# A decoder layer on one core: residual kept with its channels on the partitions up to the router, output projection with the weights stationary, half of the second shift and scale computed on VectorE

## The chip, the core and the metric

One core of a Trainium2 chip runs the whole layer for 256 tokens in one launch. Its engines are TensorE (PE, matrix products into the accumulator memory PSUM; its weight loads are listed as PEld), VectorE (DVE), ScalarE (ACT), GpSimd (POOL) and SyncE (SP, which here only issues transfers). Each runs its own instructions in a fixed order and waits for the others by semaphores. The metric is the device time of one execution in microseconds.

## What is computed

```python
mod = silu(c) @ w_ada + b_ada                      # 2048 -> 6 x 2048
sh1, sc1, g1, sh2, sc2, g2 = split(mod, 6)
h = rmsnorm(x, norm1_g) * (1 + sc1) + sh1          # x: 256 x 2048, f32
proj = h @ w_in                                    # 2048 -> 4928
o_a = hgrn2(...)                                   # gated recurrence, 8 heads, chunks of 64
o_b = latent_attention(...)                        # 8 heads, low-rank q and kv, causal
mix = concat(o_a, o_b) @ w_out                     # 2048 -> 2048
x = x + g1 * mix
h2 = rmsnorm(x, norm2_g) * (1 + sc2) + sh2
y = moe(h2)    # top 1 of 4 groups, top 2 of 8 experts in it; silu(h2 @ gate) * (h2 @ up) @ down
x = x + g2 * y
```

All inputs and weights are f32. Products on the way to the router are made as three products of rounded parts (hi x hi, hi x lo, lo x hi), each weight tile being split into a rounded part and a rest on the chip.

## The kernel before

**Weights.** All large weights come as chunks of up to 2 MB (128 partitions x 4096 columns) through one ring of slots, in one order that is written down as a list of items (lines 104 to 132). `ring_fill` (line 172) issues the next chunk on SP whenever a slot is free. The ring has four slots at first, two more after the second output-projection item (`close_temps`), and one more when the split buffers are given back. The items in order: chunks of w_ada for the first shift and scale (`ad1`, then `adt`) between those of w_in (`wh`, `win`), low-rank weights (`qup`, `kvup`), w_out (`wout`, two halves of the contraction by four blocks of 512 columns), and 192 expert chunks. The 32 chunks of w_ada for g1, sh2, sc2 and g2 (`ada`) are strewn between the last w_in items and the w_out items: `SPREAD` says how many go behind each, and what is left at the end (three chunks of g2) goes behind the first two expert chunks (`HEAD`).

**Shift and scale.** An `ada` chunk is multiplied on PE, with one column of silu(c) stationary, into four rows of one accumulator (line 293, tile `pada`, 16 matmuls a chunk). `ada_end` turns a finished row into columns on the partitions by four transposes (`pcol`), or adds it to a row (line 302, `brows`) for g1 and g2; g1 then goes out to memory and back to be broadcast over the partitions into `gate`. An `adt` chunk holds transposed weights: DVE multiplies it by silu(c), broadcast in `gate`, and sums along the row (line 271, two instructions of 128x2048 per chunk, each overwriting the chunk's half).

**First norm.** x is loaded with tokens on the partitions (four tiles of 512 channels by two blocks of tokens). `norm1` sums squares along the row, makes one reciprocal root per token (tile `sm`) and scales x by this column (line 337). `make_h` transposes 256 channels at a time on PE (`pxT`, line 382), applies shift and scale on ACT as per-partition operands (`h`, line 385) and splits the result into `hhi` and `hlo` (lines 388, 389).

**Products.** `dense` (line 411) takes for each 128 rows of weights one of four split buffers: ACT writes the rounded part (line 417), DVE the rest (line 418). Then PE runs, by default, six matmuls with activations stationary and 512 weight columns streaming (lines 432 to 434), into one PSUM bank per block of tokens; in the `turned` form, used for some w_in blocks, twelve matmuls with 128 weight columns stationary and 256 tokens streaming (lines 425 to 427), whose results have channels on the partitions. Each call takes two of the four PSUM banks with the tag "w" (tile `pacc`).

**Recurrence and attention.** `hgrn(0)` and `hgrn(1)` handle four heads each; their outputs go through transposes (`pmt`) into the two parts `mhi` and `mlo` of the output projection's input. `ptr` on PE waits for `d` (line 513), a step of the recurrence on DVE.

**Output projection.** `w_out` runs eight items of eight k-tiles. The first half's results are copied to `mix0` (line 578); the second half adds to it, multiplies by g1 and adds to x (lines 582 to 584), which was loaded again. `x2_ready` squares the result, transposes it on PE (`px2T`) and multiplies it by the router's weights (line 640, `plog`), which `router_weights` has scaled by the second norm's gain and scale; the shift enters by a sum of 16 products on 36 columns (line 614).

**Router and experts.** After the last item come the reciprocal root, the logits (line 879), the choice of experts on small tiles, their ranks by matmuls (`prank`), and the gather of tokens by one-hot matmuls (`pgat`, line 970). Then each round takes 32 token slots of an expert through gate/up (`pgu`, line 1040) and down (`py`, line 1016).

An order of all instructions on each engine is made when the kernel is built; `high_priority(-120)` at line 270 sets the 128x2048 products back behind other work in it.

## Time and profile before

| | us |
|---|---|
| runs | 1504.66, 1507.17, 1507.49 (median 1507.17) |
| the profiled execution | 1505.27 |
| its span in the trace | 1503.0 |
| first matmul of the input projection | 31.46 |
| last matmul of the output projection begins | 545.20 |
| first expert matmul | 571.41 |

Some 2.3 us of the execution lie outside the span. Over the span PE is busy for 75%, DVE for 39%, ACT for 23%, and 575.6 MB move at 383 GB/s; these are means over stages of different kinds. Busy times of PE overlap in the trace (the end of a matmul is modelled), so the distance between starts says more than the length of one. [...]

### The profile page before, as it was taken

Reading aid. Unit: us, or ns where it says so; the run is one execution under the profiler, and the core shown is the slowest. Engines: PE = TensorE matmul, PEld = TensorE weight load, DVE = VectorE, ACT = ScalarE, POOL = GpSimd, SP = SyncE. Lnnn points to the kernel's source line nnn. Section 1 sums busy time; section 2 is a strip of 40 time slices with the busy share of each in tenths; the row PEclk is TensorE's granted clock in tenths of the full one; section 3 lists DMA queues with packets and bytes.
Section 4 is the critical chain, followed back from the end, with each engine's and each line's share of the span. In section 5 each row is a group of like instructions: output and inputs, shape, how many; then the busy total and the mean of one; then the engine's idle time right before and its main releaser. Section 6 shows DMA issues by size and latency. Waiting matters only on the chain.

```text
span 1503.0 us, 22846 instructions
## 1 busy us (share of the span) xinstructions
PE 1127.9 (75%) x9893; PEld 687.8 (46%) x9893; DVE 588.6 (39%) x1200; ACT 338.4 (23%) x699; POOL 5.0 (0%) x9
## 2 busy tenths in 40 slices
PE   5989999979999989675666666657657756666556
PEld 2868887737568756333323323323423423332222
DVE  4699998769765552220120121113112112112112
ACT  5634446536435423000100100100100100000000
POOL 0000000000000000000000000000000000000000
PEclk7999999989999999888888888879888889779787
DMA  9788796877979798999999999999999999999995
GB/s 373 263 332 356 298 352 257 315 302 313 369 293 376 293 373 343 430 429 430 430 430 430 430 430 429 429 431 430 430 430 430 430 431 430 430 429 429 431 430 222
DMA packets 44143, 575.61 MB, mean 383 GB/s; under 512 B 4858, under 2 KB 5114, under 8 KB 8712
## 3 DMA queue, kind: packets, MB, share of 16 engines
q1 hardware_dynamic: 42496, 570.56, 91.4%
q10 hardware_dynamic: 1544, 3.56, 0.6%
q8 instruction: 79, 1.29, 0.3%
q14 instruction: 24, 0.20, 0.0%
HBM read 572.00 MB, written 2.11 MB: 382 GB/s over the span
## 4 chain that ended last, share of the span: by engine, by line
DMA 51%; PE 37%; DVE 9%; ACT 1%; issue 1%; SPq 0%; ACTq 0%; DVEq 0%
DMA wch<-in_w_gu_dram 37%; DMA wch<-in_w_down_dram 13%; PE pgu L1040 5%; PE pacc L433 5%; PE pacc L434 5%; PE pacc L432 5%; PE pada L293 3%; PE py L1016 3%; PE pcmb L993 2%; PE pgat L970 2%; DVE wch L271 2%; DVE split L418 2%; DVE proj L457 1%; PE pacc L427 1%; PE pacc L425 1%; PE pacc L426 1%
## 5 line engine op out<-in xcount | busy, mean ns | idle before, releaser
L1040 PE MATMUL pgu<-wch,XT 128*32 128x256 f32 x4096 | 309.7, 455 | 201.0 <-DMA wch<-in_w_gu_dram 201.0
L1040 PEld LDWEIGHTS pgu<-wch,XT 128*32 128x32 f32 x4096 | 139.2, 126 | 361.0 <-DMA wch<-in_w_gu_dram 253.9
L1016 PE MATMUL py<-wch,hT 128*32 128x256 f32 x2048 | 167.9, 485 | 76.8 <-DMA wch<-in_w_down_dram 72.1
L1020 DVE TENSOR_TENSOR Y<-py,gate 32x256 f32<-32x256 f32 x256 | 107.6, 420 | 216.5 <-PE py L1016 213.6
L1005 DVE TENSOR_TENSOR hid<-sgu,pgu 128x128 f32<-128x128 f32 x32 | 9.2, 287 | 462.2 <-ACT sgu L1003 462.2
L418 DVE TENSOR_TENSOR split<-wch,split 128x512 fp32r<-128x512 f32 (+2 forms) x248 | 159.5, 666 | 69.6 <-ACT split L417 69.0
L417 ACT ACTIVATE split<-wch 128x512 fp32r<-128x512 f32 (+2 forms) x248 | 148.0, 614 | 161.2 <-PE pacc L434 98.4
L1016 PEld LDWEIGHTS py<-wch,hT 128*32 128x32 f32 x2048 | 78.9, 133 | 155.0 <-issue 60.8
L1003 ACT ACTIVATE sgu<-pgu 128x128 f32<-128x128 f32 x32 | 8.9, 277 | 602.5 <-PE pgu L1040 602.5
L975 ACT ACTIVATE XT<-pgat,sh,a 128x128 f32<-128x128 f32 x128 | 48.1, 456 | 223.1 <-PE pgat L970 223.0
L433 PE MATMUL pacc<-split,hhi 128*128 128x512 f32 (+1 forms) x192 | 75.5, 393 | 7.0 <-DVE split L418 7.0
L425 PE MATMUL pacc<-hhi,split 128*128 128x256 f32 x256 | 72.4, 286 | 2.8 <-ACT hhi L388 2.2
L426 PE MATMUL pacc<-hlo,split 128*128 128x256 f32 x256 | 72.7, 285 | 1.7 <-DVE hlo L389 1.7
L434 PE MATMUL pacc<-split,hlo 128*128 128x512 f32 (+1 forms) x192 | 73.7, 386 | 0.0
L432 PE MATMUL pacc<-split,hhi 128*128 128x512 f32 (+1 forms) x192 | 72.9, 392 | 0.8 <-DVE proj L457 0.7
L427 PE MATMUL pacc<-hhi,split 128*128 128x256 f32 x256 | 72.2, 285 | 1.1 <-DVE split L418 1.1
L293 PE MATMUL pada<-wch,ca 128*1 128x512 f32 x512 | 68.7, 602 | 3.3 <-DVE pada L288 3.3
L993 PE MATMUL pcmb<-Y,pwt 128*128 128x512 f32 x128 | 59.2, 605 | 15.5 <-DVE Y L1020 15.5
L970 PEld LDWEIGHTS pgat<-ohr,x 128*128 128x128 f32 x512 | 63.4, 205 | 10.7 <-issue 9.8
L970 PE MATMUL pgat<-ohr,x 128*128 128x128 f32 x512 | 66.8, 291 | 0.7 <-DVE sm L937 0.7
L271 DVE SCALAR_TENSOR_TENSOR wch<-wch,gate 128x2048 f32<-128x2048 f32 x24 | 54.8, 2284 | 0.0
L457 DVE TENSOR_TENSOR proj<-proj,pacc 128x512 f32<-128x512 f32 (+1 forms) x80 | 51.2, 662 | 0.8 <-PE pacc L434 0.4
(311 smaller groups left out, 1215.4 us busy)
## 6 DMA issues: line engine op xcount, KB each, us to landing
wch<-in_w_gu_dram SPq DMA_DIRECT2D x128, 2048.0 KB, 31.1
wch<-in_w_down_dram SPq DMA_DIRECT2D x64, 2048.0 KB, 31.5
wch<-in_w_ada_dram SPq DMA_DIRECT2D x36, 2048.0 KB, 10.1
wch<-in_w_ada_t_dram SPq DMA_DIRECT2D x12, 2048.0 KB, 7.9
wch<-in_w_in_dram SPq DMA_DIRECT2D x12, 2048.0 KB, 9.2
wch<-in_w_out_dram SPq DMA_DIRECT2D x8, 2048.0 KB, 9.5
wch<-in_w_in_h_dram SPq DMA_DIRECT2D x8, 1024.0 KB, 8.9
wch<-in_w_in_dram SPq DMA_DIRECT2D x3, 1664.0 KB, 7.0
```

Source lines behind the costliest of these rows:

```text
L293: PE.matmul(acc[b][32 * j:32 * j + 1, :], ca[:, kt:kt + 1], w[:, o:o + 512], start=kt == 0, stop=kt == 15)
L417: S.activation(s[:, 0, :ncol], w, AF.Copy)
L418: V.tensor_sub(s[:, 1, :ncol], w, s[:, 0, :ncol])
L426: PE.matmul(o, s[:, 0, c], lo, start=False, stop=False, skip_group_check=True)
L432: PE.matmul(o, hi[:, c], s[:, 0, :ncol], start=first, stop=False)
L433: PE.matmul(o, hi[:, c], s[:, 1, :ncol], start=False, stop=False)
L434: PE.matmul(o, lo[:, c], s[:, 0, :ncol], start=False, stop=stop)
L970: PE.matmul(ps[:, 128 * i:128 * i + 128], x2[kt // 4][:, t, 128 * (kt % 4):128 * (kt % 4) + 128], ohr[:, t], start=t == 0, stop=t == 1)
L993: PE.matmul(ps, PWT[G4][:, 128 * t:128 * t + 128], Y4[j // 2][:, 512 * (j % 2):512 * (j % 2) + 512], start=True, stop=True)
L1016: PE.matmul(py[32 * j:32 * j + 32, :256], H["T"][:, 32 * kt:32 * kt + 32], w[:, 1024 * kt + 256 * j:1024 * kt + 256 * j + 256], start=kt = ...
L1020: V.tensor_mul(Y[q][r:r + 32, 256 * j:256 * j + 256], py[32 * j:32 * j + 32, :256], gate[32 * j:32 * j + 32, c:c + 256])
L1040: PE.matmul(gu[32 * j:32 * j + 32, :256], XT[G4][kt // 8][:, kt % 8, 32 * e4:32 * e4 + 32], w[:, 1024 * i + 256 * j:1024 * i + 256 * j + 2 ...
```

## The change

x comes transposed (`xT`), so that channels lie on the partitions from the load to the router. `norm1` squares on ACT and DVE, adds the four tiles up, sums over the partitions by two matmuls with a tile of ones, and multiplies x by a row of reciprocal roots, broadcast along the free dimension. `make_h` has no transposes left and works in place.

The output projection uses the `turned` form. After each item, of either half, four instructions (line 581 of the new kernel) take 256 columns each from PSUM, multiply by g1 (now a column per channel block) and add to the residual `xt`, which is loaded in the first half. `mix0`, the broadcast g1 and the trip of g1 through memory are gone.

Of sh2 and sc2, channels 0 to 1023 are computed on PE as before, as eight chunks `m2` that hold both; channels 1024 to 2047 come as eight transposed chunks `at2`, each multiplied on DVE by two instructions of 128x2048, and stand last in the list: two behind the first w_out item, one behind each of the next six. The g2 chunks stand before them, and none is left behind the experts. The router's weights are scaled, and its shift summed, in four steps of four k-tiles.

The sum of squares for the second norm is made on ACT and DVE and finished by ten small matmuls into the logits' bank. The rows of x2, which the gather and the end need, are rebuilt by 32 transposes and eight ACT copies after the logits (`x2_rows`).

Lines left out, removed ones for the most part, are marked by "...".

```diff
-SPREAD = (1, 4, 7, 5, 5, 2, 0, 0, 0, 2, 1, 1, 0)
+SPREAD = (1, 4, 7, 5, 5, 3, 1, 1, 1, 1, 1, 1, 0)
-HEAD = 2
...
-    mods = [("ada", b, ch) for b in ("g1", "sh2", "sc2", "g2") for ch in range(8)]
+    mods = [("ada", b, ch) for b in ("g1", "m2", "g2") for ch in range(8)] + [("at2", kt) for kt in range(8, 16)]
-    g2 = list(late_mods)
+    assert not list(late_mods)
-    items += experts[:HEAD] + g2 + experts[HEAD:]
+    items += experts
...
-    xx = [tmp([P, 2, 512], "x") for _ in range(4)]
+    xx = [tmp([P, 4, 256], "x") for _ in range(4)]
-        nc.sync.dma_start(xx[j], A["x"][:, :, 512 * j:512 * j + 512])
-    ring["limit"] = 1
+        nc.sync.dma_start(xx[j], A["xT"][:, 4 * j:4 * j + 4])
+    ring["limit"] = 3
...
+    def adt_chunk(it, sh, a, b, gain):
+        w = ring_get(it)
+        i = it[1]
         r = sm(2, "adt")
         for k in range(2):
             wk = w[:, 2048 * k:2048 * k + 2048]
             with tc.high_priority(-120):
                 V.scalar_tensor_tensor(wk, wk, 1.0, gate, op0=OP.mult, op1=OP.mult, accum_out=r[:, k:k + 1])
...
+        ring_done(it)
+        mod_shift(sh[:, i:i + 1], r[:, 0:1], b + i, 1)
+        mod_scale(a[:, i:i + 1], r[:, 1:2], b + 16 + i, gain + i, 1)
     def ada_end(b):
...
+        if b == "g2":
             for j in range(4):
                 V.tensor_add(brow[32 * j:32 * j + 1], brow[32 * j:32 * j + 1], acc[b][32 * j:32 * j + 1])
...
+            return
+        S.activation(rows, acc[b], AF.Copy)
+        pt = pm("pcol")
+        for i in range(4):
+            PE.transpose(pt[:, 128 * i:128 * i + 128], rows[:, 128 * i:128 * i + 128], ident)
+        t = sm(16)
+        V.tensor_copy(t.rearrange("p (j s) -> p s j", j=4), pt.rearrange("p (s q) -> p s q", s=4)[:, :, 0:128:32])
+        if b == "g1":
+            mod_shift(g1, t, P_BA + 64, 16)
         else:
...
+            mod_shift(sh2[:, 0:8], t[:, 0:8], P_BA + 32, 8)
+            mod_scale(a2[:, 0:8], t[:, 8:16], P_BA + 48, P_N2, 8)
+    def norm1():
+        sq = [big([P, 1024], "sq") for _ in range(4)]
+        flat = [x.rearrange("p a b -> p (a b)") for x in xx]
+        for j in range(4):
+            if j < 2:
+                S.activation(sq[j], flat[j], AF.Square)
             else:
...
+                V.tensor_mul(sq[j], flat[j], flat[j])
+        V.tensor_add(sq[0], sq[0], sq[1])
+        V.tensor_add(sq[2], sq[2], sq[3])
+        V.tensor_add(sq[0], sq[0], sq[2])
+        V.tensor_add(sq[1][:, :512], sq[0][:, :512], sq[0][:, 512:])
+        ps = pm("pss")
+        for i in range(2):
+            PE.matmul(ps[:, :256], ones, sq[1][:, 256 * i:256 * i + 256], start=i == 0, stop=i == 1)
+        ms, y, t = sq[2][:, 0:256], sq[2][:, 256:512], sq[2][:, 512:768]
+        V.tensor_scalar(ms, ps[:, :256], 1.0 / D, EPS, op0=OP.mult, op1=OP.add)
+        S.activation(t, ms, AF.Ln)
+        S.activation(y, t, AF.Exp, scale=-0.5)
+        V.tensor_mul(t, y, y)
+        V.tensor_mul(t, t, ms)
+        V.tensor_scalar(t, t, -0.5, 1.5, op0=OP.mult, op1=OP.add)
+        V.tensor_mul(y, y, t)
         for j in range(4):
...
+            for r in range(2):
+                v = xx[j][:, 2 * r:2 * r + 2]
+                V.tensor_mul(v, v, bc(y[:, None, :], [P, 2, 256]))
     posf = sm(2)
...
-        h32 = tmp([P, 2, 256], "h32")
-        ps = pm("pxT")
-        for i in range(2):
-            for t in range(2):
-                c = 256 * i + 128 * t
-                d0 = 128 * (2 * r + i)
-                PE.transpose(ps[:, c:c + 128], xx[q][:, t, d0:d0 + 128], ident)
+        sl = slice(2 * r, 2 * r + 2)
-            S.activation(h32[:, i], ps[:, 256 * i:256 * i + 256], AF.Identity, scale=a1[:, kt:kt + 1],
-                         bias=sh1[:, kt:kt + 1])
-        sl = slice(2 * r, 2 * r + 2)
-        S.activation(hi[:, sl], h32, AF.Copy)
-        V.tensor_sub(lo[:, sl], h32, hi[:, sl])
+            h = xx[q][:, 2 * r + i]
+            S.activation(h, h, AF.Identity, scale=a1[:, kt:kt + 1], bias=sh1[:, kt:kt + 1])
+        S.activation(hi[:, sl], xx[q][:, sl], AF.Copy)
+        V.tensor_sub(lo[:, sl], xx[q][:, sl], hi[:, sl])
...
             return hi[:, kt % 4], lo[:, kt % 4]
         def end(ps):
...
+            for h in range(4):
+                m = xt[j][:, h]
+                V.scalar_tensor_tensor(m, ps[h // 2][:, 256 * (h % 2):256 * (h % 2) + 256], g1[:, 4 * j + h:4 * j + h + 1],
+                                       m, op0=OP.mult, op1=OP.add)
+            if half:
+                xt_ready(j)
+        if half == 0:
+            xt[j] = big([P, 4, 256], "xt")
+            nc.sync.dma_start(xt[j], A["xT"][:, 4 * j:4 * j + 4])
+        dense(ring_get(it), 512, range(8), lhs, end, turned=True)
         ring_done(it)
...
+    xt, x2 = {}, {}
     wr2 = {}
     def router_load():
         wr2["w"] = big([P, 16, 36], "wr")
         S.dma_start(wr2["w"], A["w_r"])
+        v = cpool.tile([P, 36], F32, name="rv")
+        V.memset(v, 0.0)
+        wr2["v"] = v
+        wr2["t"] = []
     def router_begin():
         wr2["ps"] = pm("plog")
...
+    def router_weights(q):
+        wr, v = wr2["w"], wr2["v"]
+        if q % 2 == 0:
+            wr2["t"].append(big([P, 8, 128], "wr2"))
+            G.memset(wr2["t"][-1], 0.0)
+        k = slice(4 * q, 4 * q + 4)
+        V.tensor_mul(wr2["t"][q // 2][:, 4 * (q % 2):4 * (q % 2) + 4, :36], wr[:, k], bc(a2[:, k, None], [P, 4, 36]))
+        for kt in range(4 * q, 4 * q + 4):
             V.scalar_tensor_tensor(v, wr[:, kt], sh2[:, kt:kt + 1], v, op0=OP.mult, op1=OP.add)
+        if q < 3:
+            return
         ps = pm("prb")
         PE.matmul(ps[:, :36], ones, v, start=True, stop=True)
         rb = cpool.tile([P, 36], F32, name="rb")
         V.tensor_add(rb, ps[:, :36], pr[:, R_B:R_B + 36])
         wr2["b"] = rb
...
+    def xt_ready(j):
         for i in range(4):
             kt = 4 * j + i
             for t in range(2):
...
+                PE.matmul(wr2["ps"][:, 128 * t:128 * t + 128], xt[j][:, i, 128 * t:128 * t + 128], wr2["t"][kt // 8][:, kt % 8],
                           start=kt == 0 and t == 0, stop=kt == 15, skip_group_check=True)
+        if j < 3:
+            sq = big([P, 4, 256], "sq2")
+            S.activation(sq, xt[j], AF.Square)
+            if j == 0:
+                wr2["sq"] = sq
+                return
+            V.tensor_add(wr2["sq"], wr2["sq"], sq)
+            if j == 2:
+                s = wr2["sq"]
+                V.tensor_add(s[:, 0:2], s[:, 0:2], s[:, 2:4])
+                V.tensor_add(s[:, 0], s[:, 0], s[:, 1])
+            return
+        s = wr2["sq"]
+        for i in range(3):
+            S.activation(s[:, 1 + i], xt[j][:, i], AF.Square)
+        sq = big([P, 256], "sq2")
+        V.tensor_mul(sq, xt[j][:, 3], xt[j][:, 3])
+        ps = wr2["ps"]
+        for i in range(5):
+            for t in range(2):
+                PE.matmul(ps[:, 256 + t:257 + t], (s[:, i] if i < 4 else sq)[:, 128 * t:128 * t + 128], ones[:, 0:1],
+                          start=False, stop=i == 4, skip_group_check=True)
+    def x2_rows(j):
+        x2[j] = big([P, 2, 512], "x2")
+        for t in range(2):
+            ps = pw("px2")
+            for i in range(4):
+                PE.transpose(ps[:, 128 * i:128 * i + 128], xt[j][:, i, 128 * t:128 * t + 128], ident)
+            S.activation(x2[j][:, t], ps, AF.Copy)
     def mla_pre():
         qa, kva = proj.pop(0), proj.pop(1)
...
-        ("ada", "sc2", 7): router_weights,
+        ("ada", "m2", 7): lambda: (router_weights(0), router_weights(1)),
+        ("at2", 11): lambda: router_weights(2),
+        ("at2", 15): lambda: router_weights(3),
...
-    V.tensor_reduce(ms, ss2.rearrange("p (t j) -> p t j", t=2), AX.X, OP.add)
-    V.tensor_scalar(ms, ms, 1.0 / D, EPS, op0=OP.mult, op1=OP.add)
+    V.tensor_scalar(ms, wr2["ps"][:, 256:258], 1.0 / D, EPS, op0=OP.mult, op1=OP.add)
+    for j in range(4):
+        x2_rows(j)
...
-    for it in g2:
-        ada_chunk(it[1], it[2])
```

**VectorE at the start.** Rows of before, from the last step of the reciprocal root (L202) on; `x` are the four tiles, `sh` and `a` the first shift and scale, `pcol` the columns that PE made of the first two chunks:

```order
L202 TENSOR_TENSOR sm_173<-sm_173,sm_175 128x2
L337 TENSOR_SCALAR x_89<-x_89,sm_173 128x512 x2
L337 TENSOR_SCALAR x_90<-x_90,sm_173 128x512 x2
L337 TENSOR_SCALAR x_91<-x_91,sm_173 128x512 x2
L337 TENSOR_SCALAR x_92<-x_92,sm_173 128x512 x2
L418 TENSOR_TENSOR split_221<-wch_104,split_221 128x512
...
L277 TENSOR_TENSOR sh_131<-pcol_33_199,pc 128x2
L280 TENSOR_TENSOR a_132<-pcol_33_199,pc 128x2
L249 MEMSET pad_49_279 128x512
L281 SCALAR_TENSOR_TENSOR a_132<-a_132,pc 128x2
```

The same place after; `pss` is the sum over the partitions, L344 the last step of the reciprocal root, L348 the multiplication by its row:

```order
L338 TENSOR_SCALAR sq_156<-pss_166 128x256
...
L344 TENSOR_TENSOR sq_156<-sq_156 128x256
L422 TENSOR_TENSOR split_211<-wch_103,split_211 128x512
L348 TENSOR_TENSOR x_91<-x_91,sq_156 128x512 x2
L348 TENSOR_TENSOR x_92<-x_92,sq_156 128x512 x2
L348 TENSOR_TENSOR x_93<-x_93,sq_156 128x512 x2
L348 TENSOR_TENSOR x_94<-x_94,sq_156 128x512 x2
L283 TENSOR_TENSOR sh_134<-pcol_25_195,pc 128x2
L286 TENSOR_TENSOR a_135<-pcol_25_195,pc 128x2
L422 TENSOR_TENSOR split_226<-wch_103,split_226 128x512
L287 SCALAR_TENSOR_TENSOR a_135<-a_135,pc 128x2
```

The multiplication stands in both ahead of `sh` and `a`; the root's steps have grown from 2 to 256 columns, and all but one split stand behind it.

**VectorE between the first and the second output-projection item.** Before: from the last step of `mlo`, the input's second part, to the first splits of the second item (`wch_3862`):

```order
L470 SCALAR_TENSOR_TENSOR mlo_3799<-pmt_3807,pc,mhi_3798 128x4x128
L288 MEMSET pada_3991 128x512
L314 COPY sm_3959<-pcol_3954 128x4x4
L618 TENSOR_TENSOR rb<-prb_3987,pr 128x36
L280 TENSOR_TENSOR a_134<-sm_3959,pc 128x16
L281 SCALAR_TENSOR_TENSOR a_134<-a_134,pc 128x16
L609 TENSOR_TENSOR wr_679_3963<-wr_2821,a_134 128x8x36
...
L418 TENSOR_TENSOR split_4005<-wch_3862,split_4005 128x512
L418 TENSOR_TENSOR split_4014<-wch_3862,split_4014 128x512
```

After: `wch_3818` and `wch_3828` are the first two `at2` chunks, `pada_3507` is the accumulator of g2, `pacc_3832` and `pacc_3833` are the banks of the first item, `split_3994` is the second item's first:

```order
L474 SCALAR_TENSOR_TENSOR mlo_3765<-pmt_3773,pc,mhi_3764 128x4x128
L277 SCALAR_TENSOR_TENSOR wch_3818,adt_3974<-wch_3818,gate 128x2048 x2
L307 TENSOR_TENSOR brow_105<-brow_105,pada_3507 1x512 x4
L283 TENSOR_TENSOR sh_136<-adt_3974,pc 128x1
L286 TENSOR_TENSOR a_137<-adt_3974,pc 128x1
L277 SCALAR_TENSOR_TENSOR wch_3828,adt_3982<-wch_3828,gate 128x2048
L581 SCALAR_TENSOR_TENSOR xt_3830<-pacc_3832,g_138,xt_3830 128x256 x2
L581 SCALAR_TENSOR_TENSOR xt_3830<-pacc_3833,g_138,xt_3830 128x256 x2
...
L277 SCALAR_TENSOR_TENSOR wch_3828,adt_3982<-wch_3828,gate 128x2048
L615 SCALAR_TENSOR_TENSOR rv<-wr_2769,sh_136,rv 128x36
...
L422 TENSOR_TENSOR split_3994<-wch_3958,split_3994 128x512
```

Four 128x2048 instructions, the adds that finish g2 and the first item's four multiply-adds now stand ahead of the second item's splits; before, small steps did.

**VectorE at the fifth item** (second half, first block). After; `wch_4129` is its weights, `pacc_4141` and `pacc_4142` are the banks of the third item, which the fifth uses again, and `wch_4134` is an `at2` chunk:

```order
L422 TENSOR_TENSOR split_4425<-wch_4129,split_4425 128x512
L422 TENSOR_TENSOR split_4440<-wch_4129,split_4440 128x512
L422 TENSOR_TENSOR split_4455<-wch_4129,split_4455 128x512
L422 TENSOR_TENSOR split_4470<-wch_4129,split_4470 128x512
L613 TENSOR_TENSOR wr_689_4277<-wr_2769,a_137 128x4x36
L277 SCALAR_TENSOR_TENSOR wch_4134,adt_4561<-wch_4134,gate 128x2048
L581 SCALAR_TENSOR_TENSOR xt_4139<-pacc_4141,g_138,xt_4139 128x256 x2
L581 SCALAR_TENSOR_TENSOR xt_4139<-pacc_4142,g_138,xt_4139 128x256 x2
L283 TENSOR_TENSOR sh_136<-adt_4561,pc 128x1
L277 SCALAR_TENSOR_TENSOR wch_4134,adt_4561<-wch_4134,gate 128x2048
```

Before, the eight splits of this item stand in a row without anything between them, and ACT emptied the banks. Now the banks of the third item are emptied behind four splits of the fifth and one 128x2048 instruction.

## Rows read from the trace of the kernel before

**Rows 1.** Windows by stage: window, length, busy time (instructions) by engine, clock, DMA share, GB/s

```profile
0.00:31.50 31.50, 15.75 (x53) 4.66 (x53) 15.89 (x53) 15.41 (x30) 1.16 (x5) 0.82 0.92 361
...
126.00:213.00 87.00, 85.29 (x545) 75.59 (x547) 84.28 (x137) 40.16 (x67) 0.00 (x0) 1.00 0.83 321
...
449.70:545.60 95.90, 95.84 (x480) 72.06 (x480) 50.95 (x78) 41.54 (x73) 0.00 (x0) 1.00 0.86 342
...
545.60:571.40 25.80, 20.32 (x119) 11.64 (x116) 15.13 (x60) 6.70 (x20) 0.00 (x0) 0.80 0.83 336
...
571.40:1503.00 931.60, 607.97 (x6801) 305.62 (x6800) 172.02 (x387) 65.69 (x190) 0.00 (x0) 0.85 0.98 420
```

**Rows 2.** Timeline of SP around 555: start, time, queue, line, tile, issues

```profile
554.96 22.62 SPq L172 DMA_DIRECT2D wch<-in_w_gu_dram  x3
```

**Rows 3.** Timeline of startup: start us, length us, engine, line, operation, count, idle before

```profile
16.77 0.63 ACT L328 ACTIVATE junk<-x 128x512 f32<-128x512 f32 x1 [0.30 <-DMA x<-in_x_dram]
...
21.35 3.26 DVE L337 TENSOR_SCALAR x<-x,sm 128x512 f32<-128x512 f32 x8
...
29.73 1.02 ACT L385 ACTIVATE h<-pxT,sh,a 128x256 f32<-128x256 f32 x2 [1.60 <-DVE a L281]
...
31.46 0.80 PE L425 MATMUL pacc<-hhi,split 128*128 128x256 f32 x2 [2.25 <-ACT hhi L388]
```

**Rows 4.** Groups by form, 432 to 571.4: busy us, mean ns, idle before, releaser

```profile
L418 DVE TENSOR_TENSOR split<-wch,split 128x512 fp32r<-128x512 f32 x63 | 43.0, 689 | 40.4 <-ACT split L417 40.4
...
L417 ACT ACTIVATE split<-wch 128x512 fp32r<-128x512 f32 x61 | 38.2, 631 | 52.3 <-PE pacc L434 49.0 <-issue 2.6 <-DVE split L418 0.7
...
L582 DVE TENSOR_TENSOR mix<-mix,pacc 128x512 f32<-128x512 f32 x8 | 5.3, 682 | 2.1 <-PE pacc L434 2.1
...
L302 DVE TENSOR_TENSOR brows<-brows,pada 1x512 f32<-1x512 f32 x4 | 2.7, 684 | 0.7 <-PE pada L293 0.6
...
L556 DVE TENSOR_TENSOR o<-o,sm 128x1024 f32<-128x1024 f32 x1 | 1.2, 1224 | 0.0
```

**Rows 5.** Costliest groups of the whole span (page, part 5)

```profile
L1040 PE MATMUL pgu<-wch,XT 128*32 128x256 f32 x4096 | 309.7, 455 | 201.0 <-DMA wch<-in_w_gu_dram 201.0
...
L1020 DVE TENSOR_TENSOR Y<-py,gate 32x256 f32<-32x256 f32 x256 | 107.6, 420 | 216.5 <-PE py L1016 213.6
```

**Rows 6.** Timeline of PE from the last projection matmul to the gather

```profile
545.52 4.45 PE L293 MATMUL pada<-wch,ca 128*1 128x512 f32 x34
...
549.90 1.09 PE L632 MATMUL px2T<-cst,x 128*128 128x128 f32 x8
...
551.89 2.05 PE L640 MATMUL plog<-wr,x2T 128*128 128x128 f32 x16
...
566.02 5.46 PE L970 MATMUL pgat<-ohr,x 128*128 128x128 f32 x32 [0.66 <-DVE sm L937]
```

**Rows 7.** Groups by form, 126 to 213: the products of ada chunks on VectorE

```profile
L271 DVE SCALAR_TENSOR_TENSOR wch<-wch,gate 128x2048 f32<-128x2048 f32 x13 | 29.7, 2284 | 0.0
```

**Rows 8.** Waits of PE, 31.4 to 432: total us, times, longest us

```profile
PE pmt L824 <- DVE o L818: 5.4, 2, 4.6
...
PE ptr L520 <- DVE d L513: 5.1, 1, 5.1
```

**Rows 9.** Window behind the wait of pmt, columns as in the first group

```profile
309.00:315.00 6.00, 2.68 (x12) 1.63 (x16) 5.80 (x9) 3.38 (x4) 0.00 (x0) 0.50 0.96 406
```

**Rows 10.** Windows of equal length, instructions of the tile pacc alone

```profile
455.00:466.20 11.20, 11.20 (x50) 9.02 (x49) 0.00 (x0) 1.20 (x2) 1.00 0.98 394
...
127.00:138.20 11.20, 11.20 (x97) 11.20 (x96) 2.00 (x4) 0.00 (x0) 1.00 0.81 310
```

**Rows 11.** Timeline around the second output-projection item, PE and then DVE

```profile
444.49 1.90 PE L293 MATMUL pada<-wch,ca 128*1 128x512 f32 x16
...
447.23 0.48 DVE L288 MEMSET pada<- 128x512 f32 x1 [6.06 <-ACT rows L309]
...
449.28 2.49 DVE L418 TENSOR_TENSOR split<-wch,split 128x512 fp32r<-128x512 f32 x4
```

More of the change, by code (lines that the diff above doesn't have):

```diff
@@ L94, in tile_hybrid_layer @@
     ident = cst[:, C_ID:C_ID + 128]
-    ones = cst[:, C_ONE:C_ONE + 128]
+    ones = cpool.tile([P, 128], F32, name="ones")
+    G.memset(ones, 1.0)
     tri64 = cst[:, C_TRI64:C_TRI64 + 128]
@@ L145, in source @@
         if k == "ada":
-            return A["w_ada"][("g1", "sh2", "sc2", "g2").index(it[1]), it[2]], 4096
+            return A["w_ada"][("g1", "m2", "g2").index(it[1]), it[2]], 4096
+        if k == "at2":
+            return A["w_ada_t2"][it[1] - 8], 4096
         if k == "win":
@@ L241, in tile_hybrid_layer @@
     a2 = cpool.tile([P, 16], F32, name="a2")
+    g1 = cpool.tile([P, 16], F32, name="g1")
     def ad1_chunk(h, c):
@@ L574, in end @@
         def end(ps):
-            if half == 0:
-                mix0[j] = big([P, 2, 512], "mix0")
-                for t in range(2):
-                    S.activation(mix0[j][:, t], ps[t], AF.Copy)
-                return
-            m = mix0.pop(j)
-            for t in range(2):
-                V.tensor_add(m[:, t], m[:, t], ps[t])
-                V.tensor_mul(m[:, t], m[:, t], gate[:, 512 * j:512 * j + 512])
-                V.tensor_add(x2[j][:, t], x2[j][:, t], m[:, t])
-            x2_ready(j)
-        if half:
-            x2[j] = big([P, 2, 512], "x2")
-            nc.sync.dma_start(x2[j], A["x"][:, :, 512 * j:512 * j + 512])
-        dense(ring_get(it), 512, range(8), lhs, end)
+            for h in range(4):
[8 more added lines that the diff above has]
+        dense(ring_get(it), 512, range(8), lhs, end, turned=True)
         ring_done(it)
-    x2, mix0 = {}, {}
-    ss2 = cpool.tile([P, 8], F32, name="ss2")
+    xt, x2 = {}, {}
     wr2 = {}
@@ L850, in tile_hybrid_layer @@
         elif it[0] == "adt":
-            adt_chunk(it[1])
+            adt_chunk(it, sh1, a1, P_BA, P_N1)
+        elif it[0] == "at2":
+            adt_chunk(it, sh2, a2, P_BA + 32, P_N2)
         elif it[0] == "ada":
@@ L948, in gate_rows @@
             ps = pw("pg2")
-            PE.matmul(ps, ones[32 * j:32 * j + 1, :], brows[32 * j:32 * j + 1, 1], start=True, stop=True, tile_position=(32 * j, 0))
+            PE.matmul(ps, ones[32 * j:32 * j + 1, :], brow[32 * j:32 * j + 1], start=True, stop=True, tile_position=(32 * j, 0))
             S.activation(gate[:, 512 * j:512 * j + 512], ps, AF.Copy)
```

96 lines of the change are left out of this document (17 added, 79 removed).

## The prediction

> **What bounds the kernel now.** First the windows by stage [rows 1]. In the expert stage the DMA engines are busy for 0.98 of the time at 420 GB/s: it ends when the last weight has come. Ahead of it the DMA share is 0.83 to 0.92, and PE is busy for 85.29 of 87 us in the input projection and for 95.84 of 95.9 in the output projection: that half is the engines'. What joins the two is in [rows 2]: from 554.96 SP has 22.62 us for three 2 MB chunks, because every ring slot comes to hold an expert chunk until the first expert matmul frees one. So whatever moves the first expert matmul (571.41) moves the end by as much: both versions hold seven expert chunks by then, and read the same bytes. I therefore sum only up to that point, in order of time. The profiled execution took 1505.27 us, the median of the runs is 1507.17, so I carry the sum over to both. About 0.2% (3 us) is what a measurement of this kernel can tell from no change.
>
> **Startup.** Before, the last part of x is there at 16.77; the eight scalings by a column end at 24.6, and the wait ends with the modulation: h at 29.73, first matmul at 31.46 [rows 3]. The change makes the sum of squares run across partitions and the scale a row. On DVE, behind the last x: three 128x1024 operations at 1.22 and one of 512 columns at 0.69 (lines 556 and 582 in [rows 4]), with small ones 22.1; the two sums by matmul, not seen in the trace: between 0.9 (two at the 0.455 of a 256-column f32 matmul [rows 5]) and 1.8 (the same at half the clock); I take 1.7, since the granted clock is below full here (0.82 over the window [rows 1]) → 23.8. Then rsqrt on 256 columns instead of 2: five DVE operations near 0.42 [rows 5] and two on ACT near 0.5 with hand-overs, → 27.7. Eight scalings are now products with a broadcast row, 0.62 each in a row (as four splits in 2.49 [rows 11]), where the column form took 0.41 (3.26 for eight): with a split ahead of them 33.4. The shift and scale of the first chunk stand behind all eight in DVE's order: 34.6. h and hhi take 1.7 as before: first matmul at 36.2. **+4.7** (+3.5 to +6). PE has no long gap in the next 30 us that could absorb it.
>
> **Input projection.** The 32 transposes of h go; eight transposes take 1.09 [rows 6], so about 4 us of PE. But in 126 to 213 DVE is busy for 84.28 of 87 us [rows 1], and its work there (splits, 13 products of 128x2048 at 2284 ns [rows 7]) stays. **-1.5** (-3 to 0).
>
> **Attention.** In 265 to 320 PE waits 4.6 us at once for o of the first recurrence half [rows 8]. The four adds on one partition (0.684 each [rows 4], 2.7) that finish g1 stood in that DVE chain and are gone from it; one ada chunk (1.83) fills part of the gap. [...] Against that, DVE gets three router-vector steps and two products ahead of d, on which the 5.1 us wait of ptr rests [rows 8]: +2. **-2.7** (-5 to +1).
>
> **Output projection.** Two things change. Weights become the stationary operand: 12 matmuls of 256 columns per k-tile for 6 of 512. The trace has both forms: 97 of the narrow kind in 11.2 us, 50 of the wide kind in 11.2 us [rows 10]. Twice as many at half the length: 0. [...]
>
> The second thing is DVE. Half of sh2 and sc2 leaves PE (8 chunks at 1.9 [rows 11], 15 us) and becomes 16 products of 128x2048 on DVE at 2.28, two per item: 4.5 us of DVE for 1.9 of PE. The mix needs 64 multiply-adds of 256 columns from PSUM, which no row shows; the nearest, a product of 256 columns from PSUM, takes 0.42 [rows 5], and half of a 512-column one 0.34 [rows 4]; I take 0.42, 1.7 per item. Before, DVE had slack: 51 of 96 us busy, and 40.4 us idle ahead of 63 splits [rows 1, 4]. Per item it now has 8 splits (5.5) + 4.5 + 1.7 + about 1 of small ones = 12.7 against PE's 11.2.
>
> Where it starts: before, DVE had 6.06 us idle and the second item began at 449.7 [rows 11]. Now behind mlo (441.2) come one chunk (445.7), four adds that wait for PE's last g2 matmul (446.4) and take 2.7 (449.2), half a chunk (451.5), four multiply-adds (453.2), half a chunk and the small ones: first split at 456.9, first matmul at about 457. PE has only g2's chunk to do meanwhile: +7.3.
>
> From there PE alone needs 7 x 11.2 + 6 for three of four router pieces (2.05 each [rows 6]): 541.7, which is 3.9 earlier than the 545.6 of before, since it no longer does the chunks. Waits come on top. The four PSUM banks for products serve two items; the third item after needs the banks that the multiply-adds free. For the fifth item (second half, first block) PE would be ready at 492.6, but the multiply-adds stand in DVE's order behind four splits, the last of which needs the buffer that PE leaves at 492.6 (ACT 0.63, DVE 0.69 [rows 4]: 494.0), a product for the router (0.42) and half a chunk (2.3), then 4 x 0.42: 498.9, so a wait of 6.3. The same pattern at the fourth, sixth, seventh and eighth item gives 2.0, 3.1, 1.6 and 1.2. In sum 14.2: the last matmul at 556.0, +10.4. Where PE waited over 4 us the clock fell behind it (0.50 [rows 9]); of the 3 us that this costs I add 1.5, the rest lies under DVE's own work. **+12** (-4 if DVE never holds PE, +16 if each lump does).
>
> **Router.** From the last projection matmul to the start of gathering it was 20.4 us (545.6 to 566.02 [rows 6]), with 34 ada matmuls, eight transposes and the router's four adds of 0.684 in it. The transposes and adds go, ten small matmuls for the sum of squares come, and 32 transposes with eight copies rebuild the rows of x2; on ACT the copies (8 x 0.6) stand ahead of the exponentials of the selection, which costs about 2.2 on DVE's chain. By DVE's order: about 17.6. **-2.8** (-5 to 0).
>
> **Sum.** 4.7 - 1.5 - 2.7 + 12 - 2.8 = +9.7: 1515.0 from the profiled execution, 1516.9 from the median. I take 1516.
>
> **Rivals.**
> *DVE keeps ahead (faster).* If the multiply-adds and chunk products find their place in time, only the late start stays and PE runs through to 541.7: 4.7 - 1.5 - 2.7 - 3.9 - 2.8 = -6.2, 1499 to 1501. For it: DVE was idle for almost half of this stage. Against it: the order, which puts lumps of 2.3 us ahead of splits, with four split buffers (5.6 us of PE work) to cover them. It decides whether PE waits at the fifth and sixth item.
> *The gains and losses cancel (same).* Startup costs 3.5, the waits are half as long: 3.5 - 1.5 - 3.7 + 4.1 - 2.8 = about 0, 1507.
> *Lumps hold PE at every item (slower still).* If each item is paced by DVE's 12.7 to 13.1 and the clock falls behind several of the waits: stage +16, startup +6, 1523. The point is DVE's load per item over 11.2, which the counts give.
> *The narrow form is not hidden.* If a narrow matmul, with its own weight load, were held to the spacing of a wide one, each item would take 11.2 us more, eight of them 90: 1606. The row with 97 in 11.2 us, loads included, speaks against it. [...]
>
> **How the numbers follow.** Forecast (DVE's order holds PE as walked): 0.47. Faster rival: 0.25. Cancel: 0.13. Slower still: 0.13. Narrow form: 0.02. The forecast's own range is 1509 to 1521. To hold 8 in 10, I go from 1500, which takes in most of the faster rival, to 1523. Faster 0.26, same 0.13, slower 0.61.
>
> **What would show it.** Startup: first projection matmul at 35 to 37 instead of 31.46. Stage: the second item's first matmul near 457; the fifth item's first matmul waiting for DVE's multiply-add by 4 to 8 us; DVE busy for over 85% of the stage; pairs of narrow matmuls 0.12 apart. Router: 17 to 18 us from the last projection matmul to the gather. Expert stage: its length from the first expert matmul unchanged within 1 us (931.6). Wrong would be: PE busy throughout the stage (then 1500), or an expert stage that is shorter because more chunks were ready.

## The result and the profile after

The changed kernel takes 1518.43 us (median of four runs, 1516.60 to 1521.38) against 1506.97 for the kernel before: a ratio of 1.0081, 95% interval 1.006 to 1.0101. It is slower by 11.5 us where the sum forecast 9.7. The profiled execution took 1516.60 us (span 1514.8), 11.3 more than that of before; the spans differ by 11.8.

Windows of the changed kernel, with the same columns as [rows 1] and with bounds at the same events (first projection matmul, second output-projection item at full pace, last projection matmul, first expert matmul):

```profile
0.00:34.30 34.30, 16.19 (x52) 5.37 (x52) 20.98 (x43) 15.29 (x24) 1.37 (x6) 0.80 0.89 357
126.00:213.00 87.00, 85.26 (x533) 75.87 (x532) 84.51 (x134) 41.18 (x68) 0.00 (x0) 1.00 0.83 322
458.10:556.40 98.30, 89.52 (x720) 88.89 (x721) 78.75 (x136) 36.24 (x56) 0.95 (x1) 0.95 0.87 353
556.40:577.90 21.50, 18.05 (x115) 16.15 (x115) 9.92 (x52) 9.53 (x26) 0.00 (x0) 0.76 0.37 145
577.90:1514.80 936.90, 609.91 (x6802) 306.08 (x6800) 172.12 (x387) 65.76 (x189) 0.00 (x0) 0.84 0.99 417
```

Three things differ from [rows 1]. The output projection, 95.9 us from the second item on with PE busy all through, is now 98.3 us with 8.8 us of it idle, though eight chunks of PE work are gone; DVE is busy for 78.75 instead of 50.95. The router is shorter (21.5 for 25.8). And the last line is the surprise: from the first expert matmul to the end it takes 936.9 us, not 931.6. Of the 11.8 us, 6.5 were lost by the first expert matmul (571.41 to 577.94), and 5.3 after it, where the prediction had expected nothing.

The same events in the two profiled executions, from their timelines:

| event | before | after | difference |
|---|---|---|---|
| first projection matmul | 31.46 | 34.33 | +2.9 |
| last transpose of the mixers' output ends (`pmt`) | 439.44 | 440.16 | +0.7 |
| last matmul of the output projection ends | 545.59 | 556.37 | +10.8 |
| gather begins | 566.02 | 571.48 | +5.5 |
| first expert matmul | 571.41 | 577.94 | +6.5 |
| end | 1503.0 | 1514.8 | +11.8 |

What PE waits for between 440 and 560 us in the changed kernel (total, times, longest):

```profile
PE pacc L431 <- DVE split L422: 7.9, 2, 6.3
PE pacc L429 <- DVE xt L581: 7.2, 2, 5.6
PE pacc L429 <- ACT split L421: 3.2, 1, 3.2
```

That makes 18.3 us in five waits, at four of the eight items: the second, fourth, fifth and sixth. The timeline of DVE at the second item shows what stands behind the first two of them (3.2 and 6.3), and it can be laid beside the order printed ahead of the prediction:

```profile
441.81 2.28 DVE L277 SCALAR_TENSOR_TENSOR wch<-wch,gate 128x2048 f32<-128x2048 f32 x1
...
444.01 2.29 DVE L277 SCALAR_TENSOR_TENSOR wch<-wch,gate 128x2048 f32<-128x2048 f32 x1
...
447.63 2.78 DVE L307 TENSOR_TENSOR brow<-brow,pada 1x512 f32<-1x512 f32 x4 [1.32 <-PE pada L299]
...
450.59 2.29 DVE L277 SCALAR_TENSOR_TENSOR wch<-wch,gate 128x2048 f32<-128x2048 f32 x1
...
452.91 1.66 DVE L581 SCALAR_TENSOR_TENSOR xt<-pacc,g,xt 128x256 f32<-128x256 f32 x4
...
454.63 2.28 DVE L277 SCALAR_TENSOR_TENSOR wch<-wch,gate 128x2048 f32<-128x2048 f32 x1
...
457.36 2.49 DVE L422 TENSOR_TENSOR split<-wch,split 128x512 fp32r<-128x512 f32 x4
```

The chunk of g2 on PE ends at 447.6; the first split that PE needs comes at 457.36, ten microseconds later. In between DVE runs the four adds that finish g2 (2.78), the last two of four products (2.29 and 2.28), the four multiply-adds (1.66) and eight steps of under 0.3. Before, DVE had nothing to do in this stretch for 6.06 us and began its splits at 449.28 [rows 11]. PE gets a few matmuls in at 450.8, which need only ACT's part of the split; that is why the list has two waits here.

At the fifth item, DVE again:

```profile
495.08 2.50 DVE L422 TENSOR_TENSOR split<-wch,split 128x512 fp32r<-128x512 f32 x4
497.49 0.30 DVE L613 TENSOR_TENSOR wr<-wr,a 128x144 f32<-128x144 f32 x1
497.71 2.29 DVE L277 SCALAR_TENSOR_TENSOR wch<-wch,gate 128x2048 f32<-128x2048 f32 x1
...
499.92 1.66 DVE L581 SCALAR_TENSOR_TENSOR xt<-pacc,g,xt 128x256 f32<-128x256 f32 x4
```

PE has finished the fourth item at 495.35 and starts the fifth at 500.94: it wants the banks that the multiply-adds at 499.92 set free.

### The profile page after: what moved, and what is told of

Read it like the earlier page. It is cut to its first block, busy times and chain, and to the rows that moved or that the text cites. A ratio compares the mean times of both kernels' runs of the same rounds, so it can differ in the third digit from the quotient of the medians.

```text
span 1514.8 us, 23373 instructions
## 1 busy us (share of the span) xinstructions
PE 1116.8 (74%) x10141; PEld 708.8 (47%) x10141; DVE 627.1 (41%) x1259; ACT 335.9 (22%) x679; POOL 5.2 (0%) x10
## 4 chain that ended last, share of the span: by engine, by line
DMA 48%; PE 37%; DVE 12%; ACT 2%; issue 1%; ACTq 0%; DVEq 0%
DMA wch<-in_w_gu_dram 37%; DMA wch<-in_w_down_dram 10%; PE pgu L1064 6%; PE pcmb L1019 3%; PE pacc L437 3%; PE pacc L438 3%; PE pacc L431 3%; PE pacc L429 3%; PE pacc L430 3%; DVE wch L277 3%; PE pacc L436 3%; PE py L1042 3%; DVE split L422 2%; PE pada L299 2%; PE pgat L996 1%; DVE proj L461 1%
## 5 line engine op out<-in xcount | busy, mean ns | idle before, releaser
L1064 PE MATMUL pgu<-wch,XT 128*32 128x256 f32 x4096 | 317.2, 464 | 201.3 <-DMA wch<-in_w_gu_dram 201.3
L1042 PE MATMUL py<-wch,hT 128*32 128x256 f32 x2048 | 163.2, 474 | 79.3 <-DMA wch<-in_w_down_dram 74.8
L277 DVE SCALAR_TENSOR_TENSOR wch<-wch,gate 128x2048 f32<-128x2048 f32 x40 | 91.3, 2285 | 0.0
L429 PE MATMUL pacc<-mhi,split 128*128 128x256 f32 x256 | 74.2, 291 | 10.5 <-DVE xt L581 7.2
L431 PE MATMUL pacc<-mhi,split 128*128 128x256 f32 x256 | 73.5, 289 | 7.9 <-DVE split L422 7.9
L430 PE MATMUL pacc<-mlo,split 128*128 128x256 f32 x256 | 73.8, 289 | 0.0
```

The source lines that it names most:

```text
L277: V.scalar_tensor_tensor(wk, wk, 1.0, gate, op0=OP.mult, op1=OP.mult, accum_out=r[:, k:k + 1])
L429: PE.matmul(o, s[:, 0, c], hi, start=first and h % 2 == 0, stop=False, skip_group_check=True)
L430: PE.matmul(o, s[:, 0, c], lo, start=False, stop=False, skip_group_check=True)
L431: PE.matmul(o, s[:, 1, c], hi, start=False, stop=stop, skip_group_check=True)
L1042: PE.matmul(py[32 * j:32 * j + 32, :256], H["T"][:, 32 * kt:32 * kt + 32], w[:, 1024 * kt + 256 * j:1024 * kt + 256 * j + 256], start=kt = ...
L1064: PE.matmul(gu[32 * j:32 * j + 32, :256], XT[G4][kt // 8][:, kt % 8, 32 * e4:32 * e4 + 32], w[:, 1024 * i + 256 * j:1024 * i + 256 * j + 2 ...
```

## The experiments

All ratios are to the kernel before, run on the same chip in turn. Times of events are from each kernel's own profiled execution. Between two executions of the same kernel they differ by one to two and a half microseconds: in a second trace the kernel before reached the experts at 572.83 and ended at 1504.2, the changed kernel at 580.44 and 1517.4. Most of that arises before the output projection. From the end of the last `pmt` transpose to the first expert matmul two executions agree within half a microsecond: 131.98 and 132.02 us in the kernel before, 137.78 and 138.23 in the changed one. So this stretch is given as well ("from `pmt`"); it shows best what a run changes in the output projection and the router.

**Both kernels again.** No edit. 

> The kernel before, unchanged, for its trace beside the next three. Between the two profiles the span grew by 11.8 us, but the first expert matmul moved by 6.5 only (571.4 to 577.9); the other 5.3 came later, where the transfers ran at 427 GB/s instead of 430. Theory C (the rate belongs to the chip or the hour): here, next to the changed kernel, before streams at the same rate as it, and the two spans differ by 6 to 7 us. Theory K (the rate belongs to the kernel or to where its tensors lie): before streams at 430 again, beside 427 for the changed one, and the spans differ by 11 to 12 us.

> The changed kernel, unchanged. Theory C: ratio to before 1.004 (6.5 us of 1507). Theory K: 1.0075 (11.5 us). In both the first expert matmul is at 578 and the projection stage shows the waits of 3.2, 6.3, 1.5, 5.6 and 1.7 us again.

The kernel before took 1506.42 us in its one execution here, the changed kernel 1518.10 (median of five; ratio 1.008, 1.0067 to 1.0094). The window from 800 to 1200 us, where nothing but the weight stream counts, with the rate in GB/s at the end of the line, in the first trace of the kernel before:

```profile
800.00:1200.00 400.00, 260.54 (x2920) 132.85 (x2913) 72.31 (x165) 28.80 (x84) 0.00 (x0) 0.84 1.01 430
```

The same window of the changed kernel:

```profile
800.00:1200.00 400.00, 257.17 (x2884) 130.03 (x2884) 69.83 (x159) 28.87 (x84) 0.00 (x0) 0.84 1.01 427
```

The second traces read 430 and 427 as well, and the expert stage took 931.4 and 937.0 us. The spans of these two differ by 13.2 us, of which 5.6 lie in the expert stage; theory K said 11 to 12 and theory C 6 to 7. Theory C is out: the rate goes with the kernel.

**The VectorE half undone.** All 16 chunks of the second shift and scale go to TensorE, g2 last:

```diff
-    ... ("g1", "m2", "g2") ... + [("at2", kt) for kt in range(8, 16)]
+    ... ("g1", "m2", "m3", "g2") ...
```

> The changed kernel with the VectorE half of the second shift and scale undone: all 16 chunks on TensorE, g2 last. Theory (the 128x2048 products stand in VectorE's order ahead of splits and of the multiply-adds that free PSUM): the waits of 18.3 us in the output projection nearly vanish (under 4 left), eight chunks of 1.83 us come back on PE (14.6), so the first expert matmul comes 1 to 4 us earlier than in the changed kernel, at 574 to 577. Rival (the multiply-adds hold PE by themselves): over 8 us of waits stay and the first expert matmul is at 582 or later.

1516.64 us, ratio 1.0073 (1.006 to 1.0087). PE's waits between 440 and 557 us, whole list:

```profile
PE pcol L310 <- ACT rows L307: 0.7, 1, 0.7
PE prb L618 <- DVE rv L614: 0.4, 1, 0.4
```

From over 18 us to 1.1 (two short waits for other tiles), while PE got about 15 us of chunk work back. The first expert matmul is at 577.02, at the edge of the forecast 574 to 577; from `pmt` it takes 134.97 us, 3 less than in the changed kernel. So the waits do come from the products on DVE and, at the second item, from the four adds of g2 (2.78 us of the ten), which this kernel moves to the end too; the two are not separated. And moving half of the shift and scale there has bought nothing: it took some 15 us of work from PE and gave it more than that in waits.

**The startup alone.** The kernel before with the first norm of the changed one (`xT`, sums over the partitions, no `pxT`).

> The kernel before with the startup of the changed one alone: x transposed, first norm by sums over the partitions, no transposes of h. Theory: first projection matmul at 34.3 (+2.9), of which the input projection gives back about half by its missing transposes, so the first expert matmul is 1 to 2 us later than before (572.5 to 573.5), ratio 1.001. Rival (absorbed or more than given back): within 0.5 us of 571.4 or earlier. On the rate: theory K by the tensors' layout would change it here too, since an input is added.

1508.13 us, ratio 1.0019 (1.001 to 1.0028); first matmul at 34.40. The price at the start is as forecast (34.3), what becomes of it is not: the trace is 2.2 us behind the second trace of before at the first projection matmul, 1.0 at the end of the input projection, then 3.1 at the end of the last `pmt` and 3.5 at the first expert matmul (576.32), where 1 to 2 were forecast. What is lost in between is not known; two executions of one kernel lie up to 2 us apart at that `pmt` too (439.44 and 440.81 before, 440.16 and 442.21 after). Its rate is 430.

**The rate.** Where the ring slots lie in the on-chip memory is set by the sizes of the tiles allocated ahead of them. In the kernel before, six of seven slots start at byte 37632 + k x 16384 and the like, multiples of 256; in the changed one 96 bytes further on. (The seventh lies 224 bytes past a multiple of 256 in every kernel.) One unused tile among the constants moves the six, and every other tile behind it:

```diff
+    cpool.tile([P, 8], F32, name="pad")      # 32 bytes; 40 columns, 160 bytes, in e7
     gate = cpool.tile([P, D], F32, name="gate")
```

> The kernel before with one unused tile of 32 bytes per partition among the constants, nothing else. In the kernel before, six of the seven ring slots begin at a multiple of 64 bytes within a partition; in the changed kernel, whose constants are 96 bytes longer in sum, all begin 32 bytes past one. Theory S (the transfer rate in the expert stage hangs on that place): this kernel streams at 427 GB/s like the changed one, first expert matmul unchanged (571 to 573), about 5 us slower, ratio 1.0035. Rival (other causes, such as where the inputs lie in memory): 430 and ratio 1.000.

> The changed kernel with the same unused tile of 32 bytes, which brings six of its slots back to multiples of 64. Theory S: 430 GB/s in the expert stage, 5 us faster than the changed kernel, ratio to before 1.0045; first expert matmul at 578 to 580 as in the changed kernel. Rival: 427 and 1.008 again.

The kernel before, shifted by 32 bytes, reached the experts at 572.42, between the two traces of before, and took 1513.51 us, ratio 1.0046 (1.0032 to 1.0059). The changed kernel at multiples of 64 stayed at 1517.20, 1.0074 (1.006 to 1.0088). The window of the shifted kernel before:

```profile
800.00:1200.00 400.00, 259.46 (x2884) 132.59 (x2884) 71.06 (x163) 28.80 (x84) 0.00 (x0) 0.84 1.01 426
```

And of the changed kernel at multiples of 64:

```profile
800.00:1200.00 400.00, 258.45 (x2880) 130.41 (x2876) 68.94 (x157) 28.87 (x84) 0.00 (x0) 0.84 1.01 427
```

The first half of the theory held and the second did not: 64 was the wrong step. The slots of this kernel were at 37760, which is 128 past a multiple of 256. Hence:

> The changed kernel with an unused tile of 160 bytes, so that six of the seven ring slots begin at multiples of 256 bytes. Shifting the kernel before by 32 bytes took it from 430 to 427 GB/s, but bringing the changed one to multiples of 64 (which were 128 past a multiple of 256) left it at 427; the two programs that ran at 430 both have theirs at multiples of 256. Theory S2 (multiples of 256 are what counts): 430 GB/s, first expert matmul at 578 to 580, about 5 us faster than the changed kernel, ratio to before 1.0045. Rival (the shift acted in another way, and the inputs' place in memory sets the changed kernel's rate): 427 and 1.0075.

The same window again:

```profile
800.00:1200.00 400.00, 260.27 (x2900) 131.50 (x2904) 70.62 (x161) 28.81 (x84) 0.00 (x0) 0.84 1.01 430
```

1514.81 us, ratio 1.006 (1.0047 to 1.0072): 430 again, and an expert stage of 933.1 us, 3.9 less than the changed kernel's; the ratio is a little over the forecast 1.0045. The first expert matmul stayed where it was (579.84). Of all fourteen traces, the seven with slots at multiples of 256 (before twice, e3 and e7 to e10) have 931.4 to 933.1 us from the first expert matmul to the end, the seven others 936.7 to 938.6. The transfers themselves show it: the mean time of a 16 KB packet between 700 and 1400 us is 612.9 ns in each of the seven, 616.7 at 96 and at 128 bytes past a multiple, 617.7 at 32. So it is the ring's place that counts, whatever else the unused tile moves.

**Who frees the banks.** The kernel of e4_after_aligned, with ACT emptying PSUM:

```diff
-                V.scalar_tensor_tensor(m, ps[...], g1[...], m, op0=OP.mult, op1=OP.add)   # x4
+                S.activation(m[:, h], ps[...], AF.Copy, scale=g1[...])                    # x4
+            V.tensor_add(xt[j], xt[j], m)
```

> The aligned changed kernel, with ScalarE emptying PSUM after each output-projection item (four scaled copies by g1 into a tile) and VectorE adding the tile in one step of 128x1024. Theory (the wait of 5.6 us at the fifth item comes from banks that are freed behind VectorE's products): that wait and the 1.7 at the sixth fall to under 1.5 each, the 3.2 + 6.8 at the second item stays near 8 (0.5 less on VectorE); first expert matmul 5 to 7 us earlier than with the aligned kernel. Rival (the splits behind the products are what PE waits for): the 5.6 stays within 1.5 us.

PE's waits between 440 and 557 us, where `gm` is the tile that ACT fills:

```profile
PE pacc L432 <- DVE split L423: 6.6, 3, 6.0
PE pacc L430 <- ACT split L422: 3.2, 1, 3.2
PE pacc L430 <- ACT gm L582: 2.9, 2, 1.4
PE plog L630 <- DVE xt L583: 0.5, 1, 0.5
```

1514.53 us, ratio 1.0052 (1.0038 to 1.0066). The waits for the banks fall from 7.4 in two in e4_after_aligned to 2.9 in two (the fifth item's from 5.7 to 1.4) and the waits at the second item stay, as forecast. The first expert matmul comes 3.8 us earlier (574.71 for 578.54), where 5 to 7 were expected; but this execution was already 2.5 us late at the last `pmt`, and from there it gained 6.3 (131.70 for 138.02). The median is only 2.7 us lower; why so little of the 6.3 reaches the end is not shown (the expert stage of this one trace is 1.7 us longer, 938.6).

**What stands ahead of the second item.** The kernel of e4_after_aligned with another list:

```diff
-SPREAD = (1, 4, 7, 5, 5, 3, 1, 1, 1, 1, 1, 1, 0)
+SPREAD = (1, 4, 7, 5, 5, 1, 1, 1, 1, 1, 2, 2, 0)
+    mods.append(mods.pop(23))     # the last chunk of g2 goes to the end
```

> The aligned changed kernel with another list: one transposed chunk instead of two behind the first output-projection item, the others one place later, and the last chunk of g2 at the very end, so that one 128x2048 product instead of four, and no adds for g2, stand ahead of the second item's splits. Theory: the wait of 3.2 + 6.8 us at the second item falls to under 2; the load on VectorE is only moved, so 2 to 4 us of it come back as waits at the later items, and the last g2 chunk (1.8) and its adds (2.7) stand in the router; first expert matmul 1 to 6 us earlier than with the aligned kernel. Rival (VectorE's load over the stage is the bound): no gain, all 10 us come back later.

PE's waits over the same stretch:

```profile
PE pacc L431 <- DVE xt L583: 7.1, 2, 5.4
PE pacc L433 <- DVE split L424: 5.3, 4, 2.5
```

1510.55 us, ratio 1.0027 (1.0016 to 1.0039). The second item's wait is down to 0.4 us (and 0.8 at the third), the fifth item's 5.4 is untouched, and 2.5 have turned up at the eighth. The first expert matmul is 4.7 us earlier (573.83), within the forecast 1 to 6; from `pmt` the gain is 7.1 (130.97 for 138.02), and 6.7 in the medians.

**Together.** List, banks and place of the slots; then the same with the first norm of before; and, for the rest of the change alone, e2 with that norm.

> The changed kernel with the reordered list, ScalarE emptying PSUM, and slots at multiples of 256. Theory: the gains add, 4.7 (list) and 3.8 (banks) on the first expert matmul, which comes at 570 (sum of waits in the output projection under 6), and 5 in the expert stage: 1504, ratio 0.999. Rival (VectorE's load is the bound of the stage once its order is good): the second gain is half eaten, first expert matmul 573, ratio 1.001.

> As e8_all_256, with the first norm of the kernel before (tokens on the partitions, h transposed on TensorE) and the residual still read transposed. Theory (the changed startup alone costs 3.5 us at the first expert matmul): 3 to 4 us less than e8_all_256, first expert matmul at 566 to 567, 1500.5, ratio 0.997. Rival (in this program the transposes cost PE what the startup gains): within 1 us of e8_all_256.

> The kernel of e2_ada_on_pe (all chunks on TensorE) with the first norm of before and slots at multiples of 256: what is left of the change is the residual with channels on the partitions from the output projection to the router, and its weights held stationary. Theory: e2's first expert matmul of 577.0 less 3.5 is 573.5, 1 us later than before (572.8): ratio 1.000 to 1.001. Rival (the transposed residual is a gain by itself that the start hid): 569 or earlier, 0.998.

| kernel | median us | ratio (95%) | first expert matmul | from `pmt` |
|---|---|---|---|---|
| e8_all_256 | 1502.92 | 0.9983 (0.9975 to 0.9992) | 568.54 | 128.94 |
| e9_all_old_start | 1501.72 | 0.9970 (0.996 to 0.998) | 567.66 | 129.20 |
| e10_ada_on_pe_old_start | 1508.69 | 1.0014 (1.0004 to 1.0023) | 573.64 | 134.60 |

The forecast times of e8 were reached (570 and 1504), but the two gains add only in part: from `pmt`, list and banks gave 7.1 and 6.3 us alone and give 9.1 to 9.5 together (128.94 for 138.02 and, in e7, 138.43). That is nearer to the rival's mechanism than to the theory's. e9 beats both kernels, by 4.9 us the one before. PE's waits in its output projection, the whole list (e8 has the same four numbers):

```profile
PE pacc L428 <- DVE split L419: 4.0, 5, 2.3
PE plog L626 <- DVE xt L579: 3.3, 3, 2.3
PE pacc L426 <- ACT gm L578: 2.9, 2, 1.4
PE px L657 <- ACT gm L578: 0.2, 1, 0.2
```

Some 10 us are left of 18, where under 6 were forecast for e8. Between e9 and e10 stands the VectorE half, with its order and ACT's help: so arranged it is worth 5.4 us from `pmt`, 6.0 at the first expert matmul and 7.0 in the medians, where as the changed kernel has it it was worth nothing. ACT's help alone could have gained little in e10, where PE waits for 1.1 us in all in this stretch. Bringing back the old first norm gave 0.9 at the first expert matmul and 1.2 in the medians, not 3.5: here the rival held, as far as differences of this size can tell. It gains 3.5 us at the first projection matmul (30.70 for 34.17); 1.9 of them are left at the end of the input projection, in which the transposes on PE stand, and 1.1 at the end of the last `pmt`. That the transposes take it back is likely for the first part and not shown for the second.

## Why the prediction was right, and where it was not

It named the sign, the size (1516 for 1518.4) and the main cause, DVE's order in the output projection. That the number came so near is in part luck: by its own sum the first expert matmul would have come 9.7 us later. It came 6.5 later, and 5.3 came from where it had put zero.

- **Startup**, +4.7 forecast, +2.9 measured. The mechanism is right (a chain over 256 columns instead of 2, with 0.29 to 0.43 for a step on DVE, and products with a row, 4.90 for eight, for scalings by a column, 3.26 [rows 3]), its size was put too high: the first matmul is at 34.33 where 36.2 was walked. The walk was long at nearly every step (sums of squares done at 21.0 for 22.1, the root at 26.3 for 27.7, the scalings at 31.7 for 33.4); only the two sums by matmul took longer, with 2.15 us of waiting on DVE for the 1.7 taken.
- **Input projection, recurrence, attention**, -4.2 forecast, -2.2 measured (from +2.9 to +0.7; -0.6 in the second pair of traces, so the size is not firm). The wait of `pmt` for o (5.4 us in two before [rows 8]) is gone from the list of waits, as forecast, and the granted clock in 309 to 315 is 0.84 where it was 0.50 [rows 9]. But the wait for `d` grew by more than the 2 put on it: 9.0 us in two, 5.7 the longest, for 5.1 in one before [rows 8]. Of the -2.7 put on the attention, no run shows the -3.7 for the wait of `pmt` or the -1 for the clock behind it by itself.
- **Output projection**, +12 forecast, +10.1 measured (+0.7 to +10.8). This is the step that carried the prediction, and its mechanism held: second item at full pace at 458.1 (457 walked); waits of 1.5 at the fourth item (2.0), 5.6 at the fifth (6.3, though its own terms add up to 5.8), 1.7 at the sixth (3.1), none at the seventh and eighth (1.6 and 1.2). The four multiply-adds take 1.66, as taken. DVE is busy for 80% of it, not over 85%. Its size came out near because two errors offset: these waits come to 8.8 us, not 14.2, but PE's own work from 458.1 on takes 89.5 us, where 84.7 and 1.5 for the clock were put. Behind the two long waits the granted clock was 0.61 in 458.1 to 462 and 0.50 in 501 to 505.5, between the two levels that the trace has, 1.00 (full) and 0.50, at first and at 0.50 then; 34 matmuls started 0.21 us apart there instead of 0.12, by which some 3.2 us were lost, where 1.5 had been put. The rest is the next point. e2, e5 and e6 show the cause by taking it away in three ways.
- **Narrow matmuls**, 0 forecast, some +1.5 measured. They start 0.12 us apart in the trace of after too (555.73, 555.85, 555.97, 556.09), but more exactly 0.1189 on average at a granted clock of 1.00, where half of a wide one's 0.2332 is 0.1166: 0.22 us more for the 96 of an item. The counts of 97 and 50 in 11.2 us, from which the zero was read, include matmuls cut by the window's edges; the starts of the 97 lie 0.118 apart.
- **Router**, -2.8 forecast, -5.3 measured to the gather (20.4 to 15.1). About half of the 2.5 us between the two is the copies of x2 on ACT: put at 2.2 on DVE's chain, they kept DVE waiting for 1.0:

```profile
565.57 0.17 DVE L927 RECIPROCAL sm<-sm 128x2 f32<-128x2 f32 x1 [1.00 <-ACT sm L926]
```

  Where the other half lies is open. The timeline of PE from the last projection matmul on, to lay beside [rows 6]:

```profile
556.24 2.05 PE L629 MATMUL plog<-wr,xt 128*128 128x128 f32 x16
558.12 2.29 PE L651 MATMUL plog<-ones,sq 128*128 128x1 f32 x20
560.28 3.69 PE L660 MATMUL px<-cst,xt 128*128 128x128 f32 x32
563.90 2.27 PE L975 MATMUL pg<-brow,ones 1*128 1x512 f32 x8
568.04 0.63 PE L952 MATMUL prank<-sel,cst 128*128 128x32 f32 x2 [1.88 <-DVE sel L947]
...
571.48 6.54 PE L996 MATMUL pgat<-ohr,x 128*128 128x128 f32 x32 [0.56 <-DVE sm L963]
```

  The gather itself gave 1.1 of it back: 6.54 us for 5.46 [rows 6], at a granted clock of 0.56 for 0.68 over its stretch.
- **Expert stage**, 0 forecast, +5.3 measured. The failed step is "both versions hold seven expert chunks by then, and read the same bytes", from which an equal length was concluded. Same bytes, yes; but at another rate (427 GB/s for 430), because tiles allocated ahead of the ring had changed size, by 96 bytes in sum, and with them the place of the ring. The prediction's own test (931.6 within 1 us) failed at 936.9. It had not asked what lies behind those tiles in memory.

Why a transfer takes longer there was not shown: the runs moved the written end, in the on-chip memory, and give the step of 256, not a mechanism. With the ring 32, 96 and 128 bytes past a multiple of 256 the packets became 0.8, 0.6 and 0.6% longer (617.7, 616.7 and 616.7 ns for 612.9), so the loss did not grow with the distance.

## What to carry to other kernels

Work that is moved from a full engine to a half-idle one paid here only when it came in pieces that fit between what the full engine waits for: 15 us of PE work became 18 us of waits, until the long products were kept away from the splits and another engine freed the accumulators, and then the same move was worth 5 to 7 us. Ask of every long instruction on an in-order engine what stands behind it and who waits for that. And when a change alters the size of any tile that is allocated early, look at where the transfer buffers end up.
